# Projection steps beside attention in half a PSUM buffer each, in a two-layer hybrid encoder

## The chip, the cores and the metric

The program runs on one NeuronCore of a Trainium2 chip. The metric is the device time of one execution in microseconds. Three timed runs of the kernel before gave 1530.9, 1532.69 and 1532.79 us, so the median is 1532.69 us. The execution that was profiled is a fourth one; it took 1529.82 us.

## What is computed

Two layers. Each normalises its input, projects it to ten streams with one weight matrix (1024 to 3072 columns), runs three groups of attention heads on them (six differential heads, six grouped-query heads, four heads into a memory of 256 tokens), multiplies each group by a gate, projects back to 1024 columns, normalises and adds to the input.

```python
for l in range(DEPTH):                       # 2 layers, 1024 tokens, width 1024
    h = rms_norm(x, pre_norm[l])
    proj = h @ w_in[l]
    (dq, dk, dv, dgate, gq, gk, gv, ggate, mq, mgate) = jnp.split(proj, IN_OFFSETS, axis=-1)
    # A: 6 differential heads: rotary on dq, dk, two softmaxes of 1024 keys, their difference on dv
    oa = diff_attention(dq[:, :, 0], dq[:, :, 1], dk[:, :, 0], dk[:, :, 1], dv, lam)
    oa = rms_norm(oa, diff_subln[l]) * (1.0 - lambda_init) * silu(dgate)
    # B: 6 query heads on 2 key heads, q and k normalised per head, rotary by row and column
    ob = gqa_attention(gq, gk, gv) * silu(ggate)
    # M: 4 heads into 256 memory tokens
    mkv = rms_norm(mem, mem_norm[l]) @ w_mem_kv[l]
    om = softmax(mq @ mk.T * HEAD_DIM ** -0.5) @ mv * silu(mgate)
    y = jnp.concatenate([oa, ob, om], axis=-1) @ w_out[l]
    x = x + rms_norm(y, post_norm[l])
```

## The kernel before

**Staging.** A layer is built from 14 column chunks of 256 (`CHUNKS`, line 36) and 8 tiles of 128 tokens. One chunk on one tile is a *projection step*: 24 matmuls of 128 x 256 in four pieces of six (`matmul_chunk`, line 508; the matmul itself is line 518). Each value is kept as a high and a low part, so that each weight piece gives three products. Five chunks (`FIRST`) come before attention starts. The other nine (`REST`, line 55: the gates `dg0`, `dg1`, `gg0`, `gg1`, and `dq1`, `dk1`, `dv1`, `gq1`, `gq0`) are 72 steps per layer that run beside the differential heads; the generator `steps` (line 807) makes them one after the other, with the kind of buffer `st`. Then come the grouped-query and memory heads, then the output projection (line 1444).

**What follows a step.** `post` (line 752) takes the result out of PSUM. A gate is read by a tanh on ScalarE (L724) and then by a product on VectorE (L732). Values are read by ScalarE (L640) and then VectorE (L641). Queries and keys are rotated in place on VectorE (two products, L657, and a sum, L659); those with a norm are first squared on ScalarE (L676) and summed on VectorE (L684). Some columns are copied by ScalarE (L774). Later they are transposed on TensorE (L703) and copied out (L711, L712).

**Attention.** For each head a score matrix is computed twice: once for its row maxima (L1067 for the differential heads, a matmul of 512 columns into a buffer, then a reduction on VectorE, L938), and once in *units* of 1024 columns (L1077) for the exponential on ScalarE (L894), whose result is split on ScalarE and GpSimd (L898, L901) and multiplied with the values (L529 to L531, then a copy, L990).

**What sets the order.** The order of all instructions is worked out when the program is built, by a small event-driven planner (`Plan`, line 180). A process asks for an engine, a ring or a PSUM buffer, and the instruction is recorded when the planner starts it. PSUM is handed out by `Banks` (line 145): two buffers of 1024 columns (`pp0`, `pp1`) and four of 512 (`ps0` to `ps3`). `KINDS` (line 83) gives each kind of user a rank (lower first), the number it may hold at once, and the size that it takes. `st` has rank 1, at most 4 and size 1; the maxima, `mx`, rank 2, at most 4 and size 1. The planner frees a buffer when the last reader is through and knows nothing of waits inside one. The waits between engines are put in afterwards by the layer that records the instructions, from what each of them reads and writes.

Of the kernel before, what the change touches and what calls it, by code (L numbers as in the profile page):

```python
# [12 lines left out]
F32 = mybir.dt.float32  # L13
# [9 lines left out]
P = 128  # L23
# [7 lines left out]
NC = 256  # L31
# [48 lines left out]
CLOCK_WINDOW, CLOCK_LOW, CLOCK_HIGH = 3.41, 0.33, 0.85  # L80
SLACK = 0.8

KINDS = {'un': (0.5, 2, 2), 'z': (1, 2, 2), 's0': (2, 2, 1), 's1': (0, 2, 1), 'st': (1, 4, 1), 'pv': (1, 1, 1), 'tr': (-1, 2, 1), 'mx': (2, 4, 1), 'zh': (3, 2, 1)}


def raw(t):
# [3 lines left out]
class Event:  # L90
    def __init__(self, n=1):
        self.n = n
        self.waiters = []
# [9 lines left out]
class Ring:  # L103
# [16 lines left out]
    def free(self, plan, i):  # L120
        self.done.add(i)
        while self.waiters and self.ready():
            plan.push(plan.t, self.waiters.pop(0), self.take())
# [21 lines left out]
class Banks:  # L145


    def __init__(self, tiles, kinds):
        self.free_tiles = tiles
        self.kinds = kinds  # L150
        self.held = {k: 0 for k in kinds}
        self.waiters = []
        self.seq = 0
# [6 lines left out]
    def grant(self, plan):  # L160
        rest = []
        while self.waiters:
            w = heapq.heappop(self.waiters)
            _, limit, size = self.kinds[w[3]]
            if self.held[w[3]] < limit and self.free_tiles[size]:
                self.held[w[3]] += 1
                plan.push(plan.t, w[2], (w[3], size, None, self.free_tiles[size].pop(0)))
            else:
                rest.append(w)
        for w in rest:  # L170
            heapq.heappush(self.waiters, w)

    def free(self, plan, slot):
        kind, size, _, t = slot
        self.free_tiles[size].append(t)
        self.held[kind] -= 1
        self.grant(plan)

# [109 lines left out]
def trunk(ctx, tc, t_in, t_out):  # L288
# [13 lines left out]
    big = ctx.enter_context(tc.tile_pool(name="big", bufs=16))  # L302
    psp = ctx.enter_context(tc.tile_pool(name="psum", bufs=1, space=PSUM))
    banks = Banks({2: [psp.tile([P, D], F32, name=f"pp{i}") for i in range(2)],
                   1: [psp.tile([P, 512], F32, name=f"ps{i}") for i in range(4)]}, KINDS)
    R = {"rt": Ring(RT_BUFS), "wt": Ring(W_SLOTS), "big": Ring(16)}

    def open_pool(name, bufs=1, side=None):
# [3 lines left out]
    def close_pool(cm):  # L312
        cm.__exit__(None, None, None)
# [5 lines left out]
    def wait(ev):  # L319
        return "wait", ev  # L320

    def take(name):
        return "take", R[name]

    def free(name, i):
        R[name].free(pl, i)
# [48 lines left out]
    def load_piece(src, j, cols, w, col, vmax, prio=0, rt=None):  # L375

        ri = None
        if rt is None:
            ri = yield take("rt")
            rt = wr.tile([P, 2, NC], F32, name="rt")  # L380
        lst, off = [], 0
        for c0, n in cols:
            lst.append((rt[:, :, off:off + n],
                        src[j * 2 * P:(j + 1) * 2 * P, c0:c0 + n].rearrange("(a p) n -> p a n", p=P), n))
            off += n
        yield wait(dmas(lst, prio))
        if vmax is not None:
            v0, v1 = VCOLS[col]
            yield DVE(2 * (v1 - v0), lambda: dve.tensor_reduce(
                out=vmax[:, 1 + j:2 + j], in_=rt[:, :, v0:v1], axis=AX.XY, op=ALU.max, apply_absolute_value=True))  # L390
        hi, lo, wi = yield from split_w(rt)
        if ri is not None:
            free("rt", ri)
        w["t"][j] = (hi, lo, wi)
        w["ev"][j].fire(pl)
# [64 lines left out]
    def take_ps(kind):  # L460
        return "bank", banks, kind
# [46 lines left out]
    def matmul_chunk(ps, xhi, xlo, w, last, prio):  # L508

        for j in range(4):  # L510
            yield wait(w["ev"][j])
            hi, lo, wi = w["t"][j]

            def f(j=j, hi=hi, lo=lo):
                for a in range(2):
                    kt = 2 * j + a
                    for n, (x, y) in enumerate(((xhi, hi), (xhi, lo), (xlo, hi))):
                        pe.matmul(ps, lhsT=x[:, kt, :], rhs=y[:, a, :], start=(kt == 0 and n == 0),  # L518
                                  stop=(kt == KT - 1 and n == 2))

            yield PE(6 * NC, f, prio, None if j == 3 else 0.0)
            if last and wi is not None:
                free("wt", wi)
# [13 lines left out]
    def make_layer(l):  # L537
# [123 lines left out]
        def rope_lin(nat, ps, t, n, freed):  # L661
            i = yield take("ra")
            rb = Q["pj"].tile([P, NC], F32, name="rb", bufs=2)[:, :n]
            yield DVE(3 * n, lambda: rotate(nat, ps, rb, lin[:, :, t, :]), POST, ops=3)
            freed.fire(pl)
            free("ra", i)
# [140 lines left out]
        def steps(chunks, kind, prio):  # L807

            todo = []
            for c in chunks:  # L810
                todo += [(c, t) for t in range(2 if c in ("mk", "mv") else NT)]
            yield wait(opened)
            for c, t in todo:
                n = 2 if c in ("mk", "mv") else NT
                if c in ("mk", "mv"):
                    yield wait(mem_ready[t])
                    hi, lo = mT[t]
                else:
                    yield wait(L.xT_ev[t])
                    hi, lo = L.xT[t]  # L820
                yield wait(L.W[c]["ev"][0])
                nat = None
                if c in scr:
                    ni = yield take("nat")
                    nat = (Q["pj"].tile([P, NC], F32, name="nat", bufs=NAT), ni)
                slot = yield take_ps(kind)
                ps = slot[3][:, 0:NC]
                yield from matmul_chunk(ps, hi, lo, L.W[c], t == n - 1, prio)
                if c == REST[-1]:
                    if t == 0:  # L830
                        rest_on.fire(pl)
                    for s in L.xT_slot[t]:
                        free("big", s)
                if c == "mv" and t == 1:
                    close_pool(pools["mp"])
                    open_attn()
                pl.spawn(post(c, t, slot, ps, nat), pend)
# [42 lines left out]
        def open_attn():  # L880
            pools["at"], Q["at"] = open_pool(f"at{l}", side="right")
            pools["sd"], Q["sd"] = open_pool(f"sd{l}", side="right")
            sd["q"] = [Q["sd"].tile([P, S], F32R, name=f"sdq{i}") for i in range(2)]
            sd["k"] = [Q["sd"].tile([P, S], F32R, name=f"sdk{i}") for i in range(2)]
            for k, n in (("e32", E32_BUFS), ("ft", 1)):
                R[k] = Ring(n)
            at = Q["at"]
            R["e"] = Bag([tuple(at.tile([P, 1024], F16, name=f"e{x}{i}") for x in "hl") for i in range(E_BUFS)])
            R["o"] = Bag([at.tile([P, NT, 66], F32, name=f"o{i}") for i in range(O_BUFS)])
            attn_open.fire(pl)  # L890
# [768 lines left out]
        def main(nxt):  # L1659
# [9 lines left out]
            yield from open_pj()  # L1669
            first = Event(2)  # L1670
            pl.spawn(steps(FIRST[:1], "s0", 1), first)
            pl.spawn(steps(FIRST[1:2], "s1", 1.1), first)
            yield wait(first)
            yield from steps(FIRST[2:], "s0", 1)
            pl.spawn(steps(REST, "st", STP))
            ds = []
# [219 lines left out]
```

## Time and profile before

| | |
|---|---|
| median of three timed runs | 1532.69 us (1530.9 to 1532.79) |
| the profiled execution | 1529.82 us, of which its span 1528.0 us |
| TensorE (PE) busy | 1474.7 us, 97% of the span |
| VectorE (DVE), ScalarE (ACT), GpSimd (POOL) busy | 1016.4, 893.2, 907.6 us |
| projection matmuls, L518 | 642.4 us of PE, 4608 recorded |
| granted TensorE clock, mean | 0.994 |

The page shows one execution. TensorE's matmuls (PE) and its weight loads (PEld) are two rows that overlap, and the ends of matmuls are modelled, so that the duration of one matmul (286 ns in the mean) is more than the time from one to the next. The nine chunks beside the differential heads lie at about 120 to 500 us in the first layer and 865 to 1250 us in the second.

### The profile page before, as it was taken

To read this page: it belongs to the slowest core of one execution; us is meant where nothing else is said; L and a number is where in the kernel's file an instruction comes from. 1 tells how busy PE (TensorE), PEld (TensorE's weight loads), DVE (VectorE), ACT (ScalarE), POOL (GpSimd) and SP (SyncE) were. 2 spreads that over 40 slices of the span, in tenths; PEclk is the share of its full clock that TensorE was granted. 3 is DMA by queue.
4 is the path that set the end of the run, shared out by engine and by line. 5 is a ranking of instruction groups with operands and counts; after the bars stand their busy time and mean duration, and the time that the engine had idled before them with its cause. 6 is when DMAs were issued, how large, how long until landed. Compare 5 with 4: busy or idle time off the path is not lost.

```text
span 1528.0 us, 39224 instructions
## 1 busy us (share of the span) xinstructions
PE 1474.7 (97%) x15920; PEld 1366.0 (89%) x15920; DVE 1016.4 (67%) x1886; ACT 893.2 (58%) x1429; POOL 907.6 (59%) x654
## 2 busy tenths in 40 slices
PE   6999999999999999999999999999999999999997
PEld 5999999999999988887889999999999998888886
DVE  6646676777864797844566386767877748887233
ACT  5232748677668486683333347578667756686511
POOL 5033848789778495571142348469897767685400
PEclk9999999999999999999999999999999999999999
DMA  6335322233232643215255433133342246422242
GB/s 221 107 115 153 85 81 81 85 105 99 77 94 80 170 123 92 72 57 183 97 170 159 124 103 104 42 102 94 102 118 60 65 121 192 113 68 71 95 138 97
DMA packets 166658, 164.75 MB, mean 108 GB/s; under 512 B 14924, under 2 KB 140588, under 8 KB 166477
## 3 DMA queue, kind: packets, MB, share of 16 engines
q1 hardware_dynamic: 166477, 162.25, 36.3%
q8 instruction: 125, 2.05, 0.6%
q14 instruction: 56, 0.46, 0.1%
HBM read 111.74 MB, written 50.09 MB: 106 GB/s over the span
## 4 chain that ended last, share of the span: by engine, by line
PE 81%; issue 6%; DVE 5%; DMA 3%; POOL 3%; ACT 1%; SPq 1%; POOLq 0%; DVEq 0%; ACTq 0%
PE ps L518 33%; PE pp L1444 9%; PE ps L1067 6%; PE pp L1077 6%; PE ps L529 4%; PE ps L531 4%; PE ps L530 4%; PE ps L1279 3%; PE ps L1280 2%; PE pp L1291 2%; PE pp L1292 2%; DVE mx L938 1%; PE ps L476 1%; PE ps L1444 1%; POOL el L901 1%
## 5 line engine op out<-in xcount | busy, mean ns | idle before, releaser
L901 POOL TENSOR_TENSOR el<-e,eh 128x1024 f16<-128x1024 f32 x254 | 563.4, 2231 | 169.2 <-ACT eh L898 161.1
L518 PE MATMUL ps<-wt,big 128*128 128x256 f32 x4608 | 642.4, 286 | 14.4 <-DVE sl L712 3.7
L518 PEld LDWEIGHTS ps<-wt,big 128*128 128x128 f32 x4608 | 605.9, 191 | 34.9 <-DVE sl L712 4.3
L938 DVE TENSOR_REDUCE mx<-ps 128x1 f32<-128x512 f32 (+1 forms) x608 | 404.2, 684 | 118.1 <-PE ps L1067 81.2
L894 ACT ACTIVATE e<-pp 128x1024 f32<-128x1024 f32 x304 | 308.9, 1023 | 99.5 <-PE pp L1077 52.2
L898 ACT ACTIVATE eh<-e 128x1024 f16<-128x1024 f32 x264 | 277.5, 1058 | 2.9
L529 PEld LDWEIGHTS <-eh 128*128 128x128 f16 x2144 | 194.8, 96 | 13.6 <-issue 9.0
L531 PEld LDWEIGHTS <-el 128*128 128x128 f16 x2144 | 196.5, 99 | 4.7 <-POOL el L901 4.2
L530 PEld LDWEIGHTS <-eh 128*128 128x128 f16 x2144 | 196.7, 97 | 0.9 <-issue 0.8
L412 POOL TENSOR_TENSOR wt<-rt,wt 128x512 fp32r<-128x512 f32 x84 | 122.4, 1469 | 123.8 <-ACT wt L410 87.0
L454 POOL TENSOR_SCALAR u<-ss 128x1 f32<-128x1 f32 (+3 forms) x95 | 23.6, 249 | 238.2 <-DVE ss L1585 96.2
L1067 PE MATMUL ps<-sdk,sdq 96*128 96x512 f32 x384 | 159.1, 414 | 0.8 <-DVE gs L732 0.8
L529 PE MATMUL ps<-vd,eh 128*128 128x65 f16 x1536 | 151.3, 193 | 0.0
L530 PE MATMUL ps<-vd,eh 128*128 128x64 f16 x1536 | 150.4, 194 | 0.0
L531 PE MATMUL ps<-vd,el 128*128 128x65 f16 x1536 | 149.9, 192 | 0.0
L1077 PE MATMUL pp<-sdq,sdk 98*128 98x256 f32 x768 | 125.3, 285 | 0.5 <-DMA sdq<-nl 0.5
L1077 PEld LDWEIGHTS pp<-sdq,sdk 98*128 98x128 f32 x768 | 113.6, 190 | 6.1 <-issue 0.8
L990 ACT ACTIVATE o<-ps 128x130 f32<-128x130 f32 (+1 forms) x160 | 45.9, 287 | 93.8 <-PE ps L531 93.1
L1291 PE MATMUL pp<-big 128*128 128x256 f32 x384 | 98.2, 287 | 0.0
L1292 PE MATMUL pp<-big 67*128 67x256 f32 x384 | 96.7, 284 | 1.3 <-DMA big<-nl 1.3
L455 POOL TENSOR_TENSOR r<-u,mhalf 128x1 f32<-128x1 f32 (+3 forms) x95 | 80.7, 849 | 7.9
L410 ACT ACTIVATE wt<-rt 128x512 fp32r<-128x512 f32 x124 | 75.1, 629 | 15.8 <-DMA rt<-in_w_in 8.5
(244 smaller groups left out, 2628.2 us busy)
## 6 DMA issues: line engine op xcount, KB each, us to landing
rt<-in_w_in SPq DMA_DIRECT2D x96, 128.0 KB
rt<-in_w_in SPq DMA_DIRECT2D x44, 256.0 KB
gt<-g_scr SPq DMA_DIRECT2D x32, 256.0 KB
rt<-in_w_out SPq DMA_DIRECT2D x32, 256.0 KB
sdq<-s_dqa SPq DMA_DIRECT2D x48, 128.0 KB
sdk<-s_dka SPq DMA_DIRECT2D x48, 128.0 KB
big<-s_gqa SPq DMA_DIRECT2D x24, 256.0 KB
big<-s_gqb SPq DMA_DIRECT2D x24, 256.0 KB
```

The lines of the kernel that those rows point to most:

```text
L518: pe.matmul(ps, lhsT=x[:, kt, :], rhs=y[:, a, :], start=(kt == 0 and n == 0), stop=(kt == KT - 1 and n == 2))
L529: pe.matmul(o[:, 0:65], lhsT=eh, rhs=v[:, kt, 0:65], start=(kt == 0), stop=False, skip_group_check=True)
L530: pe.matmul(o[:, 0:64], lhsT=eh, rhs=v[:, kt, 66:130], start=False, stop=False, skip_group_check=True)
L531: pe.matmul(o[:, 0:65], lhsT=el, rhs=v[:, kt, 0:65], start=False, stop=(kt == n - 1), skip_group_check=True)
L894: yield ACT(1024, lambda: act.activation(e, ps, AF.Exp, scale=scale), 0, "p")
L898: yield either((ACT(1024, lambda: act.activation(eh, e, AF.Copy)), 0.0), (DVE(1024, lambda: dve.tensor_copy(out=eh, in_=e), 0, fast=True, ...
L901: (POOL(1024, lambda: pool.tensor_sub(out=el, in0=e, in1=eh)), 0.0))
L938: yield DVE(512, lambda: dve.tensor_reduce(out=out_ap, in_=src, axis=AX.X, op=ALU.max), MXP[0])
L1067: yield (512, lambda ps, n=n: pe.matmul(ps, lhsT=q()[0:96, i * P:(i + 1) * P], rhs=k()[0:96, n * 512:(n + 1) * 512], start=True, stop=True ...
L1077: pe.matmul(ps[:, a * 256:(a + 1) * 256], lhsT=k()[0:98, kt * P:(kt + 1) * P], rhs=q()[0:98, j * 256:(j + 1) * 256], start=True, stop=True)
L1291: pe.matmul(o, lhsT=ka()[:, ks], rhs=a()[:, qs], start=True, stop=False)
L1444: pe.matmul(z, lhsT=x[:, k, :], rhs=y, start=(k == KT_ORDER[0] and n == 0), stop=(k == KT_ORDER[-1] and n == 2))
```

## The change

The kind `st` gets size 0. Where a step asks for size 0, one of the free 512-column buffers is split into its two halves of 256 columns, and the step gets a half; the two halves of a buffer become a whole one again when both are free. A step may still hold one of at most four. All else is as it was; line numbers move by 8 in the first part of the file and by 9 from `max_task` on (L518 becomes L526, L659 L667, L938 L947, L1067 L1076, L1077 L1086).

```diff
-KINDS = {'un': (0.5, 2, 2), 'z': (1, 2, 2), 's0': (2, 2, 1), 's1': (0, 2, 1), 'st': (1, 4, 1), 'pv': (1, 1, 1), ...}
+KINDS = {'un': (0.5, 2, 2), 'z': (1, 2, 2), 's0': (2, 2, 1), 's1': (0, 2, 1), 'st': (1, 4, 0), 'pv': (1, 1, 1), ...}
@@ Banks.grant
             w = heapq.heappop(self.waiters)
             _, limit, size = self.kinds[w[3]]
+            if size == 0 and not self.free_tiles[0] and self.free_tiles[1]:
+                t = self.free_tiles[1].pop(0)
+                self.free_tiles[0] += [(t, 0), (t, 1)]
             if self.held[w[3]] < limit and self.free_tiles[size]:
@@ Banks.free
         self.free_tiles[size].append(t)
+        if size == 0 and (t[0], 1 - t[1]) in self.free_tiles[0]:
+            self.free_tiles[0] = [x for x in self.free_tiles[0] if x[0] is not t[0]]
+            self.free_tiles[1].append(t[0])
         self.held[kind] -= 1
@@ trunk
-                   1: [psp.tile([P, 512], F32, name=f"ps{i}") for i in range(4)]}, KINDS)
+                   1: [psp.tile([P, 512], F32, name=f"ps{i}") for i in range(4)], 0: []}, KINDS)
@@ steps
                 slot = yield take_ps(kind)
-                ps = slot[3][:, 0:NC]
+                t_ps, half = slot[3] if isinstance(slot[3], tuple) else (slot[3], 0)
+                ps = t_ps[:, half * NC:(half + 1) * NC]
```

The order of the instructions changes with it. Below, `ps_77` to `ps_80` are the four 512-column buffers, `pp_75` and `pp_76` the two of 1024; `[waits DVE_49]` means that the instruction waits for a count of VectorE's finished instructions, `Activation_49` of ScalarE's, `Pool_49` of GpSimd's, `DMAHW...` for a transfer.

PE at the start of the nine chunks in layer 0, before: the steps `dg0` on tiles 1 (`ps_80`) and 2 (`ps_78`, three of its four pieces).

```order
L518 MATMUL ps_80<-wt,big 128x256 [waits DVE_49]
L518 MATMUL ps_80<-wt,big 128x256 x23
L518 MATMUL ps_78<-wt,big 128x256 [waits DVE_49]
L518 MATMUL ps_78<-wt,big 128x256 x11
L1067 MATMUL ps_79<-sdk_1519,sdq_1517 128x512 [waits DMAHW5_49,DMAHW2_49,DMAHW6_49,DMAHW1_49,DMAHW7_49,DMAHW0_49,DVE_49]
L518 MATMUL ps_78<-wt,big 128x256 x6
```

The same place now, all in `ps_77`: the first row is the last four matmuls of tile 0 and the first six of tile 1; the row of 23 is the rest of tile 1 and the first six of tile 2; the wait for ScalarE is at the first matmul of tile 3.

```order
L526 MATMUL ps_77<-wt,big 128x256 x10
L526 MATMUL ps_77<-wt,big 128x256 [waits DVE_49]
L526 MATMUL ps_77<-wt,big 128x256 x23
L526 MATMUL ps_77<-wt,big 128x256 [waits DVE_49]
L526 MATMUL ps_77<-wt,big 128x256 x5
L1076 MATMUL ps_80<-sdk_1519,sdq_1517 128x512 [waits DMAHW5_49,DMAHW6_49,DMAHW2_49,DMAHW7_49,DMAHW1_49,DMAHW0_49]
L526 MATMUL ps_77<-wt,big 128x256 x6
L1076 MATMUL ps_78<-sdk_1519,sdq_1517 128x512
L526 MATMUL ps_77<-wt,big 128x256 x6
L1076 MATMUL ps_79<-sdk_1519,sdq_1517 128x512
L526 MATMUL ps_77<-wt,big 128x256 [waits Activation_49]
L526 MATMUL ps_77<-wt,big 128x256 x5
```

Before, each step had a buffer of its own and its one wait for an evacuation stood at its first matmul. Now neighbouring steps alternate between the halves of one buffer, and the waits for VectorE stand at the seventh matmul of tile 1 and of tile 2.

PE in the middle of the differential heads of layer 0, before: the last three pieces of a step of `gq1` in `ps_78`, and the first two pieces of the next, on tile 4, in `ps_77`.

```order
L518 MATMUL ps_78<-wt,big 128x256 x6
L1067 MATMUL ps_79<-sdk_1519,sdq_1517 128x512 [waits DVE_49]
L518 MATMUL ps_78<-wt,big 128x256 x12
L1077 MATMUL pp_75<-sdq_1518,sdk_1520 128x256 [waits Activation_49]
L1077 MATMUL pp_75<-sdq_1518,sdk_1520 128x256 x3
L703 MATMUL ps_80<-ident,nat 128x128 [waits DVE_49,Pool_49]
L703 MATMUL ps_80<-ident,nat 128x128
L518 MATMUL ps_77<-wt,big 128x256 [waits DVE_49]
L518 MATMUL ps_77<-wt,big 128x256 x5
L1067 MATMUL ps_79<-sdk_1519,sdq_1517 128x512 [waits DVE_49]
L518 MATMUL ps_77<-wt,big 128x256 x6
```

The step of `gq1` on tile 4 now, its four pieces; the step ahead of it ended in the other half of the same `ps_78`.

```order
L526 MATMUL ps_78<-wt,big 128x256 x6
L1076 MATMUL ps_79<-sdk_1519,sdq_1517 128x512 [waits DVE_49]
L526 MATMUL ps_78<-wt,big 128x256 [waits Activation_49]
L526 MATMUL ps_78<-wt,big 128x256 x5
L1076 MATMUL ps_80<-sdk_1519,sdq_1517 128x512 [waits DVE_49]
L526 MATMUL ps_78<-wt,big 128x256 [waits DVE_49]
L526 MATMUL ps_78<-wt,big 128x256 x5
L1076 MATMUL ps_77<-sdk_1519,sdq_1517 128x512
L526 MATMUL ps_78<-wt,big 128x256 x6
```

The second piece of the step now waits for ScalarE and the third for VectorE; one matmul of the maxima (L1076) stands between the pieces.

## Rows read from the trace of the kernel before

**Rows 1.** The page, its span and its engines; then the chain's shares.

```profile
span 1528.0 us, 39224 instructions
PE 1474.7 (97%) x15920; PEld 1366.0 (89%) x15920; DVE 1016.4 (67%) x1886; ACT 893.2 (58%) x1429; POOL 907.6 (59%) x654
...
PE 81%; issue 6%; DVE 5%; DMA 3%; POOL 3%; ACT 1%; SPq 1%; POOLq 0%; DVEq 0%; ACTq 0%
```

**Rows 2.** Windows of both layers: busy time by engine, granted clock, DMA.

```profile
100.00:500.00 400.00, 393.65 (x4715) 378.18 (x4714) 271.58 (x565) 260.44 (x416) 290.19 (x206) 1.00 0.33 93
850.00:1250.00 400.00, 393.88 (x4725) 378.21 (x4723) 272.97 (x567) 260.13 (x417) 291.96 (x206) 1.00 0.33 93
```

**Rows 3.** Waits of PE: us in total, times, longest.

```profile
PE ps L518 <- DVE sl L712: 3.7, 3, 1.7
PE ps L518 <- DVE vg L641: 3.2, 2, 1.6
PE ps L518 <- ACT sh L711: 3.0, 2, 1.5
PE ps L518 <- DVE nat L659: 1.5, 3, 0.9
PE ps L518 <- ACT o L990: 0.7, 2, 0.4
```

**Rows 4.** Timeline, start and duration in us: the two readers of a gate step.

```profile
124.85 0.38 ACT L724 ACTIVATE sq<-ps 128x256 f32<-128x256 f32 x1 [2.41 <-PE ps L518]
125.27 0.42 DVE L732 SCALAR_TENSOR_TENSOR gs<-sq,ps 128x256 f32<-128x256 f32 x1 [1.63 <-ACT sq L724]
```

**Rows 5.** Timeline: pieces of a step, a maximum and a rotation, 152 to 155 us.

```profile
151.44 0.40 PE L1067 MATMUL ps<-sdk,sdq 96*128 96x512 f32 x1
151.67 0.89 PE L518 MATMUL ps<-wt,big 128*128 128x256 f32 x6
152.39 0.40 PE L1067 MATMUL ps<-sdk,sdq 96*128 96x512 f32 x1
152.63 0.87 PE L518 MATMUL ps<-wt,big 128*128 128x256 f32 x6
153.34 0.39 PE L1067 MATMUL ps<-sdk,sdq 96*128 96x512 f32 x1
153.54 0.28 ACT L676 ACTIVATE sq<-ps 128x128 f32<-128x128 f32 x1 [3.13 <-PE ps L518]
153.85 0.29 DVE L657 TENSOR_TENSOR rb<-ps,lin 128x128 f32<-128x128 f32 x1 [0.42 <-ACT sq L676]
154.06 0.29 DVE L657 TENSOR_TENSOR ps<-ps,lin 128x128 f32<-128x128 f32 x1
154.38 0.29 DVE L659 TENSOR_TENSOR nat<-ps,rb 128x128 f32<-128x128 f32 x1
```

**Rows 6.** Timeline: VectorE's queue and PE's wait behind it, 229 to 235 us.

```profile
230.63 2.54 DVE L1172 SCALAR_TENSOR_TENSOR ft<-o,vc,rz 128x512 f32<-128x512 f32 x1
231.80 0.65 PE L1077 MATMUL pp<-sdq,sdk 98*128 98x256 f32 x4
233.81 0.28 DVE L712 TENSOR_TENSOR sl<-ps,sh 128x128 fp32r<-128x128 f32 x1
234.15 0.97 PE L518 MATMUL ps<-wt,big 128*128 128x256 f32 x6 [1.70 <-DVE sl L712]
```

**Rows 7.** Windows of 2 us behind that wait: the clock is the third number from the right.

```profile
234.00:236.00 2.00, 1.85 (x32) 1.81 (x33) 2.00 (x5) 1.17 (x2) 2.00 (x2) 0.86 0.11 33
236.00:238.00 2.00, 2.00 (x29) 1.90 (x27) 1.80 (x1) 0.57 (x3) 2.00 (x2) 0.50 0.00 0
238.00:240.00 2.00, 2.00 (x14) 1.93 (x13) 1.59 (x4) 1.88 (x3) 1.89 (x2) 0.78 0.23 66
```

**Rows 8.** Timeline: two readers of one buffer in a step `dv1`, 286 us.

```profile
286.13 0.27 ACT L774 ACTIVATE nat<-ps 128x128 f32<-128x128 f32 x1
...
286.43 0.35 DVE L641 SCALAR_TENSOR_TENSOR vd<-ps,vc,vd 128x128 f16<-128x128 f32 x1 [0.25 <-ACT nat L774]
```

More of the change, by code (lines that the diff above doesn't have):

```diff
@@ L81 @@
 SLACK = 0.8
-KINDS = {'un': (0.5, 2, 2), 'z': (1, 2, 2), 's0': (2, 2, 1), 's1': (0, 2, 1), 'st': (1, 4, 1), 'pv': (1, 1, 1), 'tr': (-1, 2, 1), 'mx': (2, 4, 1), 'zh': (3, 2, 1)}
+KINDS = {'un': (0.5, 2, 2), 'z': (1, 2, 2), 's0': (2, 2, 1), 's1': (0, 2, 1), 'st': (1, 4, 0), 'pv': (1, 1, 1), 'tr': (-1, 2, 1), 'mx': (2, 4, 1), 'zh': (3, 2, 1)}
 def raw(t):
```

## The prediction

> **What bounds the kernel now.** I read the page's engine line first: PE is busy for 1474.7 of 1528.0 us, and the chain that ended last is PE for 81% [rows 1]. Then the windows, to see the stage that the change touches. Over the two stretches where the nine chunks run beside the differential heads, PE is busy 393.65 of 400 us in layer 0 and 393.88 of 400 in layer 1, at a granted clock of 1.00; VectorE has about 272 of 400 us, ScalarE 260, GpSimd 291 [rows 2]. So these stages are PE's. There are 6.4 + 6.1 = 12.5 us of idle PE in them. Whatever the change does for the other engines, it can win no more than these 12.5 us there, plus what the clock lost; each microsecond in which PE stands still is lost in full, because nothing later on PE has slack to give back.
>
> Then PE's own waits. Those of projection matmuls for VectorE or ScalarE are 3.7 + 3.2 + 3.0 + 1.5 + 0.7 = 12.1 us in 12 waits, half of it in three or four waits of about 1.6 us [rows 3]. That is the kernel's present price for PSUM buffers: small.
>
> **What the change does to PE.** The work of PE is the same: the same 24 matmuls per step, the same units, maxima and value products, and their sequence is shifted only by some pieces. Nor are there more instructions on ScalarE, VectorE, GpSimd or SP's queue. What changes is where the waits stand. The planner believes that two halves are two buffers. The waits that are put in afterwards go by the whole buffer: in the order of the change the second piece of a step waits for ScalarE and the third for VectorE, while these read the other half. Of the 200 projection steps 70 now write a second half. Counting the waits of projection matmuls for a reader of their own buffer: before, 172, of which 170 at a step's first matmul, where the planner knew of them and had put work in between; now 252, of which 118 at a first matmul and 134 inside a step, where it knows nothing of them.
>
> Does a reader of one half already keep another engine out of the other half in the trace? Between two readers, yes: in a step `dv1` ScalarE copies columns 128 to 255 (L774), VectorE reads columns 0 to 127 (L641) and was idle for 0.25 us until the copy had ended [rows 8]. For a matmul against a reader before shows nothing, since no two steps shared a buffer. The Trainium skill, in "PSUM — Partial Sum Buffer", section "PSUM bank collisions raise a hardware error", says that any two engines must be kept apart by the bank, not by the address, TensorE's writes included. By that rule the waits are needed and the time comes out as below, 1618 us; were only readers kept apart, which is all that the row shows, PE would lose nothing and the time would stay at about 1530.
>
> **The price of one such wait.** It is a loop: PE ends the piece that the reader waits for, the reader starts, ends, and PE starts again. The next PE instruction could start at 153.34 and the square at 153.54 began behind the piece before it: 0.20 us from PE to a reader [rows 5]. From a reader to PE: VectorE's L712 ended at 233.81 + 0.28 = 234.09, the matmuls started at 234.15, and those six took 0.97 where six take 0.88: 0.06 + 0.09, I take 0.12 [rows 5, 6]. In between stand the reader's own times: tanh 0.38 and product 0.42 for a gate [rows 4]; for a rotation of 128 columns three operations from 153.85 to 154.67, so 0.82, with a square of 0.28 before it in some chunks [rows 5]. Rotations of 256 columns I take as half as long again. Against it counts what PE has to do in between: a piece of six takes 0.72 (151.67 to 152.39), a maximum 0.24 (152.39 to 152.63) [rows 5].
>
> Two places, worked out. Gate steps `dg0`: the product of tile 0 ends 0.20 + 0.38 + 0.04 + 0.42 behind tile 0's last matmul, and PE restarts at 1.16; it has six matmuls of tile 1 to do in that time, 0.72. Shortfall 0.44 us. Step `gq1` on tile 4: the readers of the step ahead stand behind its first piece, then come square and copy, 0.20 + 0.17 + 0.27 (they overlap), and the restart: 0.76, less one maximum, 0.24: shortfall 0.52. Then the rotation starts behind the second piece: 0.20 + 0.82 + 0.12 = 1.14, less 0.24: 0.90. Together 1.4 us in one step of 24 x 0.12 = 2.9 us.
>
> Doing this for every wait of the order, 137 of them have a loop longer than PE's work inside it:
> - 49 that end on a rotation's sum (L659): 45 us, 0.92 each;
> - 46 on a gate (32 on the tanh, 14 on the product): 22.5 us, 0.49 each;
> - 22 on a square or a copy of ScalarE: 14 us, 0.65 each;
> - 20 on values (L640, L641): 14.5 us, 0.73 each.
>
> Where two loops overlap, only the excess of the second is counted. The sum is 96 us. The same count over the order of before gives 20 waits and 13.7 us; the trace has 12.1 [rows 3], so the method comes out near what was measured. The hand-overs are the weakest part: with 0.10 and 0.08 in place of 0.20 and 0.12 it is 79 us, with 0.23 and 0.16 it is 105.
>
> **What the clock adds.** Behind the wait of 1.70 us that began at 231.80 + 0.65 = 232.45 the granted clock fell to 0.86, 0.50 and 0.78 in three windows of 2 us, that is to the lower level of 1.2 GHz for part of them [rows 6, 7]; at that level they did 2 x (0.14 + 0.50 + 0.22) = 1.7 us less work. It did so after one of the stage's longest waits; the mean of 1.00 over both stages leaves room for little more of it [rows 2]. 34 of the new waits are over 1 us, most under 1.5, and they come with work between them. I take 3 falls, 5 us; bounds 0 and 12 falls, 20 us.
>
> **Costed at nothing.** The evacuations get later by the piece they wait for; ScalarE and VectorE have 130 us to spare in 400 [rows 2], and while PE stands they catch up. If that cover is gone, the exponential behind a held reader comes late and PE waits for a 1024-column buffer; that is the rival of the queues' heads. What the maxima win by more free buffers is also put at nothing: at most the 12.5 us.
>
> **Sum.** The profiled execution took 1529.8. Its waits of 12.1 go and 96 come: +84. Clock +5. 1529.8 + 84 + 5 = 1619. The three timed runs lie 1 to 3 us above the profiled one; I leave that out and say 1618 us, 5.6% slower than the median.
>
> **The rivals.**
> - *Covered waits.* A stall delays PE and with it everything that it feeds, while readers catch up, so that a reader held once is early at the next wait; and the longest loops, which hold VectorE's queue of maxima, may be shorter than I count. Then half or less is left: 25 to 50 us, about 1568. For it: VectorE and ScalarE are idle a third of the time [rows 2]. Against: the loops are chains from PE back to PE, in which the reader has no queue to shorten, and the same count was right for before.
> - *Heads of queues.* A reader that waits for PE's piece blocks all behind it on an in-order engine. VectorE had an operation of 2.54 us in front of the L712 for which PE waited 1.70 [rows 6]; with 134 such meetings inside steps the wait grows by what stands ahead. A third on top of 96 and 20 us of clock give 1529.8 + 84 + 32 + 20 = 1666, up to 1690.
> - *Buffers win (faster).* Steps held up to four of the four 512-column buffers; in halves they mostly hold one, and maxima, transposes and value products always find a buffer. Price: the waits of 12.1 us go, and with them a fall of the clock, 1.7: 1516. It decides if the new waits together stay under 14 us, a seventh of what I count. For it: the waits of before are for buffers. Against: the 12.5 us of idle are all there is, and 134 waits inside steps stand against them.
> - *No effect.* The planner could seldom use halves; but 70 of 200 steps are in a second one. Or the waits of halves are all covered: then about 1530.
>
> **How the numbers follow.** The forecast with its neighbourhood (1590 to 1655) has 0.72, covered waits 0.13, heads of queues 0.10, buffers win 0.03, no effect 0.02. About 0.2% is what a measurement of this kernel tells from no change: the three runs differ by 0.12%. Faster 0.03, same 0.02, slower 0.95. The range that should hold 8 in 10 takes the forecast's own bounds (79 to 105 us, clock 0 to 20: 1597 to 1643), and reaches into covered waits below and heads of queues above: 1572 to 1668.
>
> **What would show it.** In the profile of the changed kernel: PE waits of L526 for DVE L667, L740, L649 and ACT L732, L684, L782, some 130 of them and 80 to 110 us in sum, where before had 12; a window of 400 us with PE busy about 350 instead of 394; readers of a step that wait for "PE ps L526" in the middle of the next step; the stages behind (grouped-query heads, output projection) as long as before. I am wrong if PE's share in these stages stays over 96%, or if PE idles there for something else than readers of its own buffer: then it is a queue, and the loop was not the price.

## The result and the profile after

The changed kernel takes 1643.84 us in the median of four runs (1639.81 to 1647.84), the kernel before 1532.68 (1530.9 to 1532.79, four runs): a ratio of 1.0728, 95% interval 1.0699 to 1.0757. It is 111 us slower. The forecast was 1618 with a range of 1572 to 1668.

The page after, its span, engines, chain and the group of the projection matmuls (busy, mean ns of one, idle before them and what ended most of it), against [rows 1]; below it the same group of the page before:

```profile
span 1643.6 us, 39269 instructions
...
PE 1520.0 (92%) x15920; PEld 1382.5 (84%) x15920; DVE 1018.8 (62%) x1890; ACT 898.4 (55%) x1433; POOL 887.4 (54%) x646
...
PE 79%; DVE 8%; issue 6%; ACT 3%; DMA 2%; POOL 1%; SPq 1%; DVEq 0%; POOLq 0%; ACTq 0%
...
L526 PE MATMUL ps<-wt,big 128*128 128x256 f32 x4608 | 664.5, 290 | 78.4 <-DVE nat L667 37.4
```

```profile
L518 PE MATMUL ps<-wt,big 128*128 128x256 f32 x4608 | 642.4, 286 | 14.4 <-DVE sl L712 3.7
```

PE has the same 15920 matmuls. The other engines' busy times are within 21 us of before, so no work was added. PE's idle time in front of projection matmuls grew from 14.4 to 78.4 us. Time in which PE is not busy grew from 1528.0 - 1474.7 = 53.3 to 1643.6 - 1520.0 = 123.6 us, by 70.3; and PE's busy time grew by 45.3 us without a matmul more. These two make the 115.6 us of the span.

The windows of the two stages after, against [rows 2] (columns: length; busy time and count of PE, PEld, DVE, ACT, POOL; granted clock; DMA share; GB/s):

```profile
100.00:500.00 400.00, 361.77 (x3939) 335.70 (x3938) 243.55 (x516) 217.79 (x359) 232.81 (x177) 0.98 0.29 81
850.00:1250.00 400.00, 362.67 (x3788) 339.33 (x3787) 246.93 (x542) 203.10 (x349) 211.11 (x174) 0.99 0.32 91
```

PE is busy 362 of 400 us where it had 394, and passes 3939 and 3788 matmuls where it passed 4715 and 4725. VectorE, ScalarE and GpSimd are busy for less of the 400 us too, so none of them got nearer to its limit; PE stands more. PE's waits say for whom, against [rows 3] (us in total, times, longest):

```profile
PE ps L526 <- DVE nat L667: 37.4, 45, 2.3
PE ps L539 <- POOL el L910: 7.4, 6, 1.8
PE ps L526 <- ACT vg L648: 7.0, 6, 1.2
PE ps L526 <- DVE gs L740: 7.0, 12, 0.9
PE ps L526 <- ACT sq L732: 6.8, 22, 0.5
...
PE ps L526 <- ACT sq L684: 5.2, 12, 1.4
...
PE ps L526 <- ACT e L903: 2.8, 2, 1.4
PE ps L526 <- ACT nat L782: 2.8, 6, 0.6
PE ps L526 <- DVE vg L649: 2.3, 6, 0.4
...
PE ps L526 <- DVE vd L649: 2.0, 2, 1.0
...
PE ps L526 <- ACT vd L648: 0.4, 2, 0.2
```

Projection matmuls that wait for a reader of steps in their own buffer (L667, L648, L649, L740, L732, L684, L782): 113 waits, 70.9 us. Before, all waits of projection matmuls for a reader of a buffer were 12 and 12.1 us, and of these only 5 waits and 4.7 us were for readers of steps (L641 and L659 in [rows 3]). Two more waits after, 2.8 us, are put down to an exponential (L903); in the first of them the rotation's sum of the same step ended at 267.85 us and PE started at 268.00, so they are probably of the same kind.

How one such wait looks: the gates `dg0`, tiles 0 to 2, the place of the prediction's first worked example, in the timeline after (start, duration; in brackets the idle time before it and what ended it):

```profile
125.37 0.38 ACT L732 ACTIVATE sq<-ps 128x256 f32<-128x256 f32 x1 [3.12 <-PE ps L526]
...
125.78 0.42 DVE L740 SCALAR_TENSOR_TENSOR gs<-sq,ps 128x256 f32<-128x256 f32 x1 [3.02 <-ACT sq L732]
...
126.26 3.13 PE L526 MATMUL ps<-wt,big 128*128 128x256 f32 x24 [0.93 <-DVE gs L740]
...
129.43 0.38 ACT L732 ACTIVATE sq<-ps 128x256 f32<-128x256 f32 x1 [3.15 <-PE ps L526]
129.84 0.42 DVE L740 SCALAR_TENSOR_TENSOR gs<-sq,ps 128x256 f32<-128x256 f32 x1 [3.18 <-ACT sq L732]
...
130.32 0.98 PE L526 MATMUL ps<-wt,big 128*128 128x256 f32 x6 [0.93 <-DVE gs L740]
```

The row of 24 matmuls at 126.26 is the last 18 of tile 1 and the first six of tile 2, which go into the other half. The tanh of tile 1 begins at 129.43, when those 24 have ended (126.26 + 3.13 = 129.39), not when the 18 have. Then tanh, product, PE, one after the other: 0.38 + 0.42 and the hand-overs, while PE stands for 0.93. The durations are those of [rows 4]; what is new is that they stand in PE's way, twice within 5 us.

The second worked place, a step of `gq1` in the timeline after:

```profile
353.55 0.29 DVE L665 TENSOR_TENSOR ps<-ps,turnq 128x128 f32<-128x128 f32 x1
353.94 0.29 DVE L667 TENSOR_TENSOR nat<-ps,rb 128x128 f32<-128x128 f32 x1
...
354.38 0.95 PE L526 MATMUL ps<-wt,big 128*128 128x256 f32 x6 [0.67 <-DVE nat L667]
```

The sum of the rotation ends at 354.23 and PE starts at 354.38. In the kernel before, the three VectorE operations of [rows 5], from 153.85 to 154.67, ran while PE went on:

```profile
153.57 0.90 PE L518 MATMUL ps<-wt,big 128*128 128x256 f32 x6
154.31 0.64 PE L1077 MATMUL pp<-sdq,sdk 98*128 98x256 f32 x4
```

The clock: the mean granted clock of the execution is 0.984, before 0.994. PE's timeline and windows of 2 us at one of the falls, against [rows 7]:

```profile
187.99 3.11 PE L526 MATMUL ps<-wt,big 128*128 128x256 f32 x24 [0.87 <-DVE nat L667]
192.45 0.98 PE L526 MATMUL ps<-wt,big 128*128 128x256 f32 x6 [1.35 <-ACT sq L684]
194.34 1.61 PE L526 MATMUL ps<-wt,big 128*128 128x256 f32 x6 [0.92 <-DVE nat L667]
```

```profile
192.00:194.00 2.00, 0.98 (x6) 0.78 (x6) 0.81 (x5) 0.28 (x1) 1.83 (x4) 1.00 0.65 194
194.00:196.00 2.00, 1.66 (x10) 1.56 (x11) 0.29 (x1) 0.00 (x0) 0.58 (x2) 0.61 0.01 3
196.00:198.00 2.00, 2.00 (x44) 2.00 (x42) 0.00 (x0) 0.00 (x0) 0.00 (x0) 0.54 0.00 0
```

Waits of 1.35 and 0.92 us follow each other; six matmuls that took 0.98 then take 1.61, and the clock is at or near the lower of its two levels (1.2 GHz) until 198. Summed over windows of 2 us behind 100 us, and without the last fall as the program ends, which both kernels have, the change lost 20.4 us in ten such places, before lost 3.4 in two. Inside the two stages, up to the first grouped-query matmul of each layer, these are 12.0 us in six places after and 1.7 in one before.

### The profile page after: what moved, and what is told of

It is laid out like the page before. It is cut to its first block, busy times and chain, and to the rows that moved or that the text cites. A ratio compares the mean times of both kernels' runs of the same rounds, so it can differ in the third digit from the quotient of the medians.

```text
span 1643.6 us, 39269 instructions
## 1 busy us (share of the span) xinstructions
PE 1520.0 (92%) x15920; PEld 1382.5 (84%) x15920; DVE 1018.8 (62%) x1890; ACT 898.4 (55%) x1433; POOL 887.4 (54%) x646
## 4 chain that ended last, share of the span: by engine, by line
PE 79%; DVE 8%; issue 6%; ACT 3%; DMA 2%; POOL 1%; SPq 1%; DVEq 0%; POOLq 0%; ACTq 0%
PE ps L526 33%; PE pp L1453 8%; PE pp L1086 4%; PE ps L1076 4%; PE ps L537 4%; PE ps L538 4%; PE ps L539 4%; PE ps L1288 3%; PE pp L1300 3%; PE pp L1301 3%; PE ps L1289 3%; DVE mx L947 2%; PE ps L1453 1%; PE ps L484 1%; DVE nat L667 1%
## 5 line engine op out<-in xcount | busy, mean ns | idle before, releaser
L910 POOL TENSOR_TENSOR el<-e,eh 128x1024 f16<-128x1024 f32 x264 | 580.6, 2210 | 297.4 <-ACT eh L907 241.5
L526 PE MATMUL ps<-wt,big 128*128 128x256 f32 x4608 | 664.5, 290 | 78.4 <-DVE nat L667 37.4
L526 PEld LDWEIGHTS ps<-wt,big 128*128 128x128 f32 x4608 | 608.9, 193 | 125.9 <-DVE nat L667 25.0
L947 DVE TENSOR_REDUCE mx<-ps 128x1 f32<-128x512 f32 (+1 forms) x608 | 401.9, 683 | 134.9 <-PE ps L1076 84.7
L903 ACT ACTIVATE e<-pp 128x1024 f32<-128x1024 f32 x304 | 309.3, 1022 | 101.9 <-PE pp L1086 54.1
L907 ACT ACTIVATE eh<-e 128x1024 f16<-128x1024 f32 x274 | 287.2, 1055 | 2.4
L537 PEld LDWEIGHTS <-eh 128*128 128x128 f16 x2208 | 202.3, 97 | 13.7 <-issue 8.7
L539 PEld LDWEIGHTS <-el 128*128 128x128 f16 x2208 | 203.9, 99 | 8.2 <-POOL el L910 8.2
L538 PEld LDWEIGHTS <-eh 128*128 128x128 f16 x2208 | 204.1, 98 | 0.9 <-issue 0.7
L420 POOL TENSOR_TENSOR wt<-rt,wt 128x512 fp32r<-128x512 f32 x76 | 106.3, 1408 | 140.0 <-ACT wt L418 96.7
L1076 PE MATMUL ps<-sdk,sdq 96*128 96x512 f32 x384 | 158.8, 414 | 2.7 <-DVE sl L720 2.2
L1086 PE MATMUL pp<-sdq,sdk 98*128 98x256 f32 x768 | 126.1, 287 | 0.1
L1086 PEld LDWEIGHTS pp<-sdq,sdk 98*128 98x128 f32 x768 | 115.1, 192 | 6.6 <-DMA sdq<-nh 0.5
L1300 PE MATMUL pp<-big 128*128 128x256 f32 x384 | 99.9, 291 | 0.0
L719 ACT ACTIVATE sh<-ps 128x256 fp32r<-128x256 f32 (+1 forms) x116 | 40.8, 352 | 78.6 <-PE ps L711 54.9
L1288 PE MATMUL ps<-big 128*128 128x512 f32 x192 | 82.3, 429 | 0.6 <-DVE mx L947 0.3
```

The source lines that it names most:

```text
L537: pe.matmul(o[:, 0:65], lhsT=eh, rhs=v[:, kt, 0:65], start=(kt == 0), stop=False, skip_group_check=True)
L538: pe.matmul(o[:, 0:64], lhsT=eh, rhs=v[:, kt, 66:130], start=False, stop=False, skip_group_check=True)
L539: pe.matmul(o[:, 0:65], lhsT=el, rhs=v[:, kt, 0:65], start=False, stop=(kt == n - 1), skip_group_check=True)
L903: yield ACT(1024, lambda: act.activation(e, ps, AF.Exp, scale=scale), 0, "p")
L907: yield either((ACT(1024, lambda: act.activation(eh, e, AF.Copy)), 0.0), (DVE(1024, lambda: dve.tensor_copy(out=eh, in_=e), 0, fast=True, ...
L910: (POOL(1024, lambda: pool.tensor_sub(out=el, in0=e, in1=eh)), 0.0))
```

## The experiments

Two theories were to be told apart. A: the loss is PE's waits for readers that still hold the other half of the buffer it writes. B: the order itself, with fewer steps in flight and late evacuations, feeds PE worse.

**Readers off the buffer, order kept** (`e1_readers_off`; `e2_before_readers_off` is the same edit in the kernel before). In both, what evacuates a step reads a table in SBUF in place of the buffer, so that the projected values are left out:

```diff
-            for k, o in enumerate((rb, ps)):
+            for k, o in enumerate((rb, nat)):
...
+                if kind == "st":
+                    ps = lin[:, 0].rearrange("p a b -> p (a b)")
                 pl.spawn(post(c, t, slot, ps, nat), pend)
```

> The changed kernel, its instructions in the same order on every engine, but the readers of the 144 steps beside attention read a constant table in SBUF instead of the step's result (and the rotation's second product is written to the output tile instead of back in place). This leaves the projected values out; every engine has as many instructions of the same sizes. No matmul then waits for a reader of a step. Theory A (the loss is PE waiting for readers of the other half of its buffer): the 111 us go, and those few that the kernel before paid for its buffers too: 1515 to 1535 us, PE waits of L526 for ACT and DVE under 5 us after the start. Theory B (the loss is the changed order: steps that hold one buffer, maxima and transposes elsewhere): the order is kept, so 1620 to 1645 us. Theory C (half of it is readers that block ScalarE's and VectorE's queues while they wait for PE): these waits go as well here, so as A; what would be left is seen at the exponential.

> The same edit in the kernel before: readers of the 144 steps read a constant table, which leaves the projected values out. It is the control of the run before. Theory A: the waits of 12 us and a fall of the clock of 1.7 us go: 1515 to 1525 us. Theory B: the same. If it is within 5 us of e1_readers_off, the changed order by itself costs nothing; if e1 is 20 us or more above it, the order has a part.

Measured: 1577.23 us (ratio to before 1.0299, 1.0284 to 1.0314) and, for the control, 1606.76 (1.0493, 1.0474 to 1.0511). The control misses: an edit that should have cost nothing cost 76 us, so e1 can't be read against before. VectorE's groups from 150 to 500 us say why, first before, then the control (busy, mean ns):

```profile
L732 DVE SCALAR_TENSOR_TENSOR gs<-sq,ps 128x256 f32<-128x256 f32 x20 | 8.3, 414 | 18.2 <-ACT sq L724 12.0 <-ACT e L894 6.2
...
L657 DVE TENSOR_TENSOR rb<-ps,lin 128x128 f32<-128x128 f32 x16 | 4.7, 291 | 9.6 <-PE ps L518 6.3 <-ACT sq L676 1.8 <-ACT vg L640 1.1
```

```profile
L657 DVE TENSOR_TENSOR rb<-lin 128x128 f32<-128x128 f32 x16 | 15.1, 946 | 0.0
L732 DVE SCALAR_TENSOR_TENSOR gs<-sq,lin 128x256 f32<-128x256 f32 x14 | 14.4, 1026 | 0.4 <-DMA g_scr<-gs 0.2
```

With both operands in SBUF a product of 128 columns took 946 ns in place of 291. The control's timeline shows one of them beside GpSimd:

```profile
202.62 2.59 POOL L903 TENSOR_TENSOR el<-e,eh 128x1024 f16<-128x1024 f32 x1
...
203.13 2.23 DVE L657 TENSOR_TENSOR rb<-lin 128x128 f32<-128x128 f32 x1
...
205.28 0.28 DVE L657 TENSOR_TENSOR nat<-lin 128x128 f32<-128x128 f32 x1
```

It began inside GpSimd's split and ended (205.36) 0.15 us after that had ended (205.21); the next, alone, took 0.28. Of the 32 first products of this form in the control, 21 began inside a GpSimd operation and took 1.27 us in the mean; the 11 others took 0.27 to 0.28. In the kernel before 22 of the same 32, with one operand in PSUM, also began inside a GpSimd operation, and none took over 0.29. The Trainium skill, "SBUF — State Buffer", section "SBUF: two separate sides", says that a VectorE operation with two SBUF inputs and a GpSimd operation that reads SBUF take a shared pair of ports, whichever starts first, for the whole instruction, and that the other is blocked. These rows agree. What is left of the pair of runs: in the same disguise the changed order is 30 us faster than the order of before, and its waits for L667 are gone. That speaks against B, but the edit had put a new cost into both, so neither theory is settled by it.

**Stand-ins without a second SBUF operand** (`e5_standins`; `e6_before_standins`, the same in the kernel before). The order stays. ScalarE's readers read a table; VectorE's become reductions of a table and memsets, with one SBUF input at most:

```diff
+    def idle_turn(nat, n):
+        for k in range(2):
+            dve.tensor_reduce(out=junk[:, k:k + 1], in_=table(n), axis=AX.X, op=ALU.max)
+        dve.memset(nat, 0.5)
...
-            yield DVE(3 * n, lambda: rotate(nat, ps, rb, lin[:, :, t, :]), POST, ops=3)
+            yield DVE(3 * n, lambda: idle_turn(nat, n) if n == 128 else rotate(nat, ps, rb, lin[:, :, t, :]), POST, ops=3)
...
-            yield ACT(NC, lambda: act.activation(th, ps, AF.Tanh, scale=0.5), POST, "p")
+            yield ACT(NC, lambda: act.activation(th, table(NC), AF.Tanh, scale=0.5), POST, "p")
```

and likewise for squares, gate products, values and copies. The projected values are left out again.

> The changed kernel, its instructions in the same order on every engine, but the readers of the 144 steps beside attention have stand-ins of about the same length that touch no PSUM: ScalarE reads a constant table; VectorE's products are reductions of that table (128 columns, 0.28 us, as L684 before) and memsets of the output. This leaves the projected values out. Unlike in e1_readers_off no VectorE operation gets two SBUF operands, which had made them two to three times as long beside GpSimd. Theory A (PE waits for readers of the other half): with all these waits gone the time is 1515 to 1540 us. Theory B (the changed order itself): 1600 us or more. Between 1545 and 1600 both have a part.

> The control of the run before: the same stand-ins in the kernel before, projected values left out. 1510 to 1530 us by both theories (waits of 12 us and a fall of the clock go, if VectorE's work is as long as before). By theory A e5_standins is within 10 us of this; what it is above this is the part of the changed order without any wait for halves.

Measured: 1517.31 us (0.990, 0.9885 to 0.9914) and 1519.21 (0.991, 0.9894 to 0.9927). Page, waits and windows of e5:

```profile
span 1515.1 us, 39103 instructions
...
PE 1473.1 (97%) x15920; PEld 1370.5 (90%) x15920; DVE 984.9 (65%) x1890; ACT 894.7 (59%) x1433; POOL 889.6 (59%) x646
```

```profile
PE ps L549 <- POOL el L919: 6.7, 6, 1.8
...
PE ps L536 <- DVE nat L678: 1.5, 3, 0.9
```

```profile
100.00:500.00 400.00, 399.34 (x4727) 385.00 (x4726) 276.05 (x591) 256.11 (x413) 275.15 (x199) 1.00 0.35 98
850.00:1250.00 400.00, 398.31 (x4741) 382.73 (x4740) 277.01 (x596) 259.73 (x414) 280.01 (x200) 1.00 0.36 99
```

The same order, the same matmuls, and PE is busy for 399 and 398 of 400 us at a clock of 1.00. Of waits for readers of the step's buffer (L678 is L667 of the change) 1.5 us are left. The span is 128.5 us shorter than the change's, and the order of the change is no worse than that of before under the same edit (1517 against 1519). So A holds and B falls for this order. The control tells what before pays for its own buffers, at most: 13 us, since the stand-ins also made VectorE's work 34 us shorter in either kernel (984.9 us in e5, 1018.8 in the change). One thing the stand-ins do not tell apart: readers that do not read the step do not wait for PE either, so what they held up in ScalarE's and VectorE's queues goes as well. For that, the trace of the change has to serve: PE's list has no wait of L1086 for the exponential. Not all that the change lost is gone with the waits: behind the differential heads (540 to 580 and 1280 to 1320 us) the clock still fell in four places, its mean is 0.988 (0.995 in the control), and the wait for GpSimd's split (L919) keeps 6.7 us.

**One kind of reader at a time.** `e7_standins_rotations` has the stand-ins for rotations and squares only, `e8_standins_rest` for gates, values and copies only.

> As e5_standins, but stand-ins for the rotations and their squares alone (chunks dq1, dk1, gq0, gq1; values of these columns left out); gates, values and plain copies read their half as in the change. The count of loops longer than PE's work goes from 96 to 38 us (before: 14). Theory A: 1531 + 111 x (38 - 14) / (96 - 14) = 1563, between 1550 and 1580 us. Theory B: 1600 us or more.

> As e5_standins, but stand-ins for the gates, the values and the plain copies alone (these values left out); rotations and squares read their half as in the change. The count is 62 us. Theory A: 1531 + 111 x (62 - 14) / (96 - 14) = 1596, between 1580 and 1612 us. Theory B: 1600 us or more. With e7: the rotations' part is larger than that of all others together by theory A, 80 against 47 us.

Measured: 1568.21 us (1.0231, 1.0211 to 1.025) and 1589.37 (1.0373, 1.0343 to 1.0404); by the medians 75.6 and 54.5 us less than the change, 130.1 together, where both edits at once gave 126.5. The kinds add up, as prices of separate loops do. The waits for PE, first of e7, then of e8:

```profile
PE ps L536 <- ACT sq L742: 7.6, 22, 1.2
PE ps L536 <- DVE gs L750: 7.0, 12, 0.9
```

```profile
PE ps L536 <- DVE nat L678: 41.5, 51, 2.3
...
PE ps L536 <- ACT sq L695: 5.6, 14, 1.4
```

The kind that was left in keeps its waits: the gates of e7 have 7.6 and 7.0 us as in the change (6.8 and 7.0). The prediction's count, done again for these orders, falls by 58 and 34 us; the times fell by 1.3 and 1.6 times as much. What comes with the waits (the clock, which is 0.994 in e7 and 0.981 in e8, and waits elsewhere) is in the times and not in the count. In e7 the clock did not fall inside the two stages at all; e8, which kept the rotations' waits, has seven falls there.

**Halves only where no whole buffer is free** (`e3_spread`). A step now takes a fresh buffer first:

```diff
-            if size == 0 and not self.free_tiles[0] and self.free_tiles[1]:
+            if size == 0 and self.free_tiles[1]:
                 t = self.free_tiles[1].pop(0)
-                self.free_tiles[0] += [(t, 0), (t, 1)]
+                self.free_tiles[0] = [(t, 0)] + self.free_tiles[0] + [(t, 1)]
```

> Halves as in the change, but a step takes a fresh whole buffer first and a second half only when no whole one is free. The order then has 52 waits for a reader of the own buffer inside a step instead of 134, and 44 second halves instead of 70. The count of loops that are longer than PE's work inside them gives 38 us, against 96 for the change and 14 for before. Theory A: the loss goes with the count: 111 x (38 - 14) / (96 - 14) = 33 us, so 1555 to 1575 us. Theory B (steps held to few buffers): steps are spread over all four buffers as in before, so within 10 us of before.

Measured: 1590.02 us (1.0379, 1.0366 to 1.0393), above the 1555 to 1575 that were expected of it by A. Waits:

```profile
PE ps L526 <- DVE nat L667: 19.9, 27, 1.5
PE ps L922 <- DVE nm L919: 13.9, 4, 6.7
```

With 52 waits inside steps in place of 134 the own-buffer waits fall as they should, and half of the loss goes. What was missed is outside the count: 13.9 us of waits of L922 (0.9 before) and a clock of 0.982. Nearly all of the 13.9 are two waits, one per layer, in the middle of the grouped-query heads. The first, with the VectorE operation that caused it:

```profile
581.23 9.24 DVE L419 TENSOR_TENSOR wt<-rt,wt 128x512 fp32r<-128x512 f32 x1
...
590.61 0.37 PE L922 MATMUL ps<-ident,nm 128*8 128x128 f32 x1 [6.44 <-DVE nm L919]
```

This VectorE operation, a split of weights with two SBUF operands, takes 1.16 us in the mean of the change. Here it lasted 9.24 us, and 9.55 in the other layer, while five GpSimd operations on SBUF followed each other from 581.13 to 589.92; L919, for which PE waited, stood behind it on VectorE. So these 13 us look like the effect that the two readers-off runs had shown, brought in by this order; without them e3 would lie at about 1577, by estimate.

**Fewer steps in flight, whole or half.** `e4_whole_2` and `e9_whole_1` are the kernel before with two and one buffers for steps; `e10_half_2` is the change with two halves:

```diff
-KINDS = {... 'st': (1, 4, 1), ...}
+KINDS = {... 'st': (1, 2, 1), ...}
```

and `(1, 1, 1)`; in the change `(1, 4, 0)` becomes `(1, 2, 0)`.

> The kernel before with one number changed: a kind of step beside attention may hold two whole buffers instead of four. No shared halves, waits only at a step's first matmul, 7 long loops of 6 us by the count against 20 and 14 us in before. Theory A: 1518 to 1533 us, no slower than before, perhaps 5 to 10 us faster. Theory B (steps that hold fewer buffers make the loss, as in the change, where they mostly hold one): 1560 us or more.

> The kernel before with one number changed: a kind of step beside attention may hold one whole buffer at a time. It then has as few buffers as the change mostly gives it, but shares none: all waits are at a step's first matmul, and the planner knows of them. Theory A (waits inside steps, unknown to the planner): well under the change; the count is 41 long loops of 38 us, so 1531 + 111 x (38 - 14) / (96 - 14) = 1563, between 1535 and 1575 us. Theory B (steps that hold only one buffer at a time make the loss): 1600 to 1640 us.

> The change with at most two steps' halves held at once instead of four: both nearly always in one buffer. 150 waits inside steps instead of 134, 151 long loops of 103 us instead of 137 of 96. Theory A: a little above the change, 1645 to 1665 us. If it is below the change by over 10 us, the number of steps in flight behind PE, not the waits inside, would set the loss.

Measured: e4 1535.11 us (1.0027, 1.0016 to 1.0038), e9 1623.23 (1.059, 1.0548 to 1.0633), e10 1642.89 (1.0711, 1.0671 to 1.0752). With two whole buffers 4 us are lost, where 5 to 10 us less had been thought possible, and nothing is won: steps hardly need four, and nobody else needs the two that come free. With two halves the time is that of the change, just under the 1645 to 1665 that the count gave. So in either kernel it matters little whether two or four steps may be open. e9 misses by far and came where B had put it. Its first waits:

```profile
PE ps L518 <- DVE nat L659: 13.6, 11, 2.9
PE ps L703 <- POOL nat L693: 13.3, 14, 2.0
PE ps L531 <- POOL el L901: 8.5, 14, 1.1
```

With one buffer the step behind can't begin before the readers are through, and the planner knows it. Yet waits elsewhere grow (L703 for GpSimd from 0.2 us before to 13.3, L531 from 3.6 to 8.5); why they do is open. So B names a real way to lose 90 us, but not this kernel's: the change's order loses nothing once its readers stay out of PSUM (e5). No kernel with all its work done beat the one before.

## Why the prediction was right

**The place and the mechanism.** Most of the time went where the prediction put it, into waits of projection matmuls for readers of their own buffer. Of the 115.6 us of span, 70.9 - 12.1 = 58.8 are idle time in these waits. PE's busy time holds a second part of the same waits: the end of a matmul is modelled, and in [rows 5] six matmuls show 0.89 where the next piece can start after 0.72, so by estimate each stall hides 0.17, and 0.09 at the restart, in busy time. For 113 - 12 = 101 waits more that is 26 us of the 45.3.

**The sum.** With 0.26 added to each wait's idle time, the classes come out against the forecast so:

| ends on | forecast: waits, us | measured: waits, idle us | with 0.26 each |
|---|---|---|---|
| a rotation's sum | 49, 45 | 45, 37.4 | 49 |
| a gate | 46, 22.5 | 34, 13.8 | 23 |
| a square or copy | 22, 14 | 18, 8.0 | 13 |
| values | 20, 14.5 | 16, 11.7 | 16 |
| all | 137, 96 | 113, 70.9 | 100 |

Fewer waits than counted, each dearer: 0.89 us in place of 0.70. Taken the same way the waits of before cost 12.1 + 12 x 0.26 = 15, so the difference is 85; the prediction had 84. That it is met so closely is in part luck: the number of waits was a fifth too high and the price a fifth too low.

**The step that was mis-sized** is the clock, and what follows a stall elsewhere. The prediction took three falls, 5 us, at the lower end of its 0 to 20. Measured: (1 - 0.984) x 1643.6 = 26.3 us of clock lost against (1 - 0.994) x 1528.0 = 9.2, so 17 more. The argument that the new waits are mostly under 1.5 us and have work between them did not hold: at 194 us the clock fell behind two such waits in a row. And PE's waits for others, put at nothing, grew too: all its listed waits rose from 46.3 to 114.8 us, by 68.5, so by 9.7 beside the steps' readers; the largest piece is GpSimd's split before a value product, 3.6 before, 7.4 after, and the next are the two waits put down to L903, 2.8. With 1.8 us of idle time that no wait names: 85 + 17 + 9.7 + 1.8 = 113.5 of the 115.6 us. How far these two follow from the waits is only in part settled. Inside the two stages the change lost 12.0 us of clock where before lost 1.7, and there e5 and e7 had no fall and e8 had seven: these 10 us go with the rotations' waits. Outside them the change lost 8.4 us and before 1.7; e5, without the waits, lost 13.7 there and kept the wait for GpSimd, so this part may belong to the order.

**The worked places.** At `gq1` the second wait, forecast at 0.90, is 0.67 of idle time and about 0.93 with what busy time hides. At `dg0` the forecast of 0.44 was wrong: 0.93, and 1.19 with the hidden part. It let PE's six matmuls of the next tile cover the loop. But the tanh, too, waits for these six, since they write its buffer: the piece that should have been cover is a part of the loop. A wait by whole buffers works in both directions, PE for the reader and the reader for PE's neighbouring piece.

**The rivals.** Covered waits (1568): no; of the 49 waits forecast on a rotation's sum 45 are there, with 0.83 us of idle time each. Heads of queues (1666): in part, by its clock of 20 us (17 measured); the measured time lies 26 us above the forecast and 22 below this rival. Its longer waits are not seen. The longest, 2.28 us at 411, is a norm's chain of 256 columns (square, sum, two products, sum, 409.31 to 411.34), with one operation of the transposes put between on ScalarE, and no long one ahead. Buffers win: no; neither e4 nor e5 shows a gain from free buffers beyond the 13 us that before pays for its own. No effect: no.

The rule of the Trainium skill ("PSUM — Partial Sum Buffer", section "PSUM bank collisions raise a hardware error") that two engines are kept apart by bank gave the forecast's side of this: with the waits by whole buffer 1618, without them 1530, measured 1643.84. The runs show what such waits cost. That the chip needs them no run here shows: the waits were never taken away with the readers left in place.

**What was to be seen.** L526's waits for the six named lines: some 130 of 80 to 110 us forecast, 113 of 70.9 found (L648 beside them). PE busy 350 of 400: 362. Readers that wait for PE in the middle of the next step: the tanh at 129.43. One sign did not come: the grouped-query heads take 200 and 203 us, from their first matmul (L1279, L1288 after) to their last (L1291, L1300), where before took 188 and 187. That belongs to the order and not to the waits, since e5 takes 201 and 202 there: the last units of the differential heads now end 30 us behind the first grouped-query matmul, before 1.2. From the last grouped-query matmul to the end of the program it is 100 us, before 99.

## What to carry to other kernels

Half a buffer is a buffer only if waits go by halves. Where they go by the whole, count the loop for every pair of neighbours, from PE through the reader and back, with the neighbour's piece inside the loop and not as its cover: here 113 waits at 0.9 us. So before a planner's resources are split, ask whether what records the waits sees the same pieces as what plans them: a wait that the planner does not know of it can't fill. That a planner which knows them does better is not shown in general; with one whole buffer (e9) it knew them all and lost 89 us.

## What had not been expected of the hardware

- A VectorE product of two SBUF operands, begun inside a GpSimd operation on SBUF, took 2.23 us in place of 0.28 and ended 0.15 us after it; in the mean 946 ns against 291 with one operand in PSUM. In the kernel before, reading the step out of PSUM keeps the rotations clear of GpSimd; the table in SBUF cost 76 us in all. In e3 another operation of two SBUF operands lasted through five GpSimd operations in a row, 9.24 us in place of 1.16.
- The busy time of PE rose by 45 us with the same matmuls: by the estimates above some 17 are clock, some 26 the modelled ends and restarts around stalls. A stall that shows 0.93 us of idle time costs about 1.2.
- The clock fell in ten places behind 100 us where it fell in two before, one of the ten after waits of 1.35 and 0.92 us with 0.98 us of matmuls between; five falls also came in e5, outside the two stages, where PE had almost none of these waits.
